# Gate matrix from one-hot products: fp32 operands against a power of two with a high and a low 16 bit part

## The chip, the cores and the metric

The kernel runs on one core of one Trainium2 chip. The metric is the device time of one execution in microseconds; the time before is the median of three runs, 961.69 us (960.93 to 962.33).

## What is computed

One decoder layer for 256 tokens of width 1024. The change lies in its last part, the product-key expert layer ("peer"). Each token gets 8 heads x 16 experts out of 128 x 128 with a gate for each:

```python
top_s, pos = lax.top_k(cand_s, PEER_TOPK)
experts = jnp.take_along_axis(cand_i, pos, axis=-1)
gates = jax.nn.softmax(top_s, axis=-1)
u = u_tab[ec]
a = jax.nn.gelu(jnp.einsum('td,thkd->thk', hc, u), approximate=False)
return jnp.einsum('thk,thkd->td', gc * a, v_tab[ec])
```

An expert's number is 128 x i1 + i2. For part of the tokens the kernel gathers the expert rows. For the others (176 of the 256) it computes all 16384 experts densely, and multiplies by a gate matrix W[i2, i1, token] that is zero except at the token's 128 experts.

## The kernel before

**Stages.** First the mixer (projections, retention, block attention, output projection), then the queries and keys of the experts, then a loop over 128 blocks of the table u (L1248 to L1282), then a loop over 128 blocks of the table v. Both tables stream through a ring of six 512 KB tiles on SyncE's queue.

**One step of the u loop** (block c): TensorE transposes block c + 2 (L737, eight 128x128 transposes), and ScalarE copies the result to SBUF (L738). TensorE multiplies block c with the hidden states (L1264, eight fp32 products of 128x128x128). Every second block ScalarE applies gelu (L1221, L1224), and GpSimd multiplies by the gates that exist by then (L1222). Then `gather` issues row fetches on GpSimd (L1028) and, a few steps later, their dots on VectorE (L1039). Last, `chain_step(BUDGET)` advances the side work by 1.5 us of its own planned costs: first the top-16 selection, then `dense_gates`, whose steps are booked with GSTEP = 1.6 each. So a group of four tokens is made for almost every block, 44 groups in all.

**A group of four tokens.** For token t let r run over its 128 (head, k) pairs on the partitions. With one-hot rows of i2 and of i1 the token's gate matrix is a product that contracts over r: W[:, :, t] = onehot(i2)^T (onehot(i1) x gate). `columns(t)` (L1170) transposes the indices and gates of 128 tokens, so that r lies on the partitions, and copies them from PSUM on ScalarE (`tT`, `tT1`). `one_hots` (L1145) builds, on VectorE, `o2`, an fp32 comparison of the negated iota with -i2 (L1152), and `o1b`, a bf16 comparison of `iota4` with i1 (L1154). Its `factors` (L1156) multiplies o1b by the gate on ScalarE, four activations for the four tokens (L1158), giving the fp32 `o1`. TensorE multiplies o2 by o1 for each token into one PSUM bank (L1192). `gates_evac` (L1201) writes the bank to W: for the blocks that are through, VectorE multiplies by what stands there (L1205), for the others ScalarE copies (L1207).

**What sets the order.** The order on each engine is that of the program (a manual schedule); engines meet at semaphores. In the step that builds group n, TensorE multiplies group n - 2 (LAG_G = 2), ScalarE makes the factors of group n - 1, and at the head of the next block the results of n - 2 are evacuated. The one-hots have three buffers in `oh_buf`, the factors and `o1b` two each, spread over `oh_buf` and `oh_more`; PSUM has two banks for the groups (`acc(1)`).

Of the kernel before, what the change touches and what calls it, by code (L numbers as in the profile page):

```python
# [11 lines left out]
F32 = mybir.dt.float32  # L12
F32R = mybir.dt.float32r
BF16 = mybir.dt.bfloat16
I16 = mybir.dt.int16
BF16 = mybir.dt.bfloat16
I32 = mybir.dt.int32
U32 = mybir.dt.uint32
AF = mybir.ActivationFunctionType
OP = mybir.AluOpType  # L20
AX = mybir.AxisListType

P = 128
S = 256
NT = S // P
D = 1024
KC = D // P
H = 8
NK = 128
# [6 lines left out]
NA = S - NG - NX  # L36
# [41 lines left out]
def layer_kernel(ctx, tc, x, mix_norm_g, w_in, ret_w_branch, moba_q_gain, moba_k_gain, moba_w_branch,  # L78
# [3 lines left out]
    V, A, G, T = nc.vector, nc.scalar, nc.gpsimd, nc.tensor  # L82
    ctx.enter_context(tc.manual_schedule())

    cp = ctx.enter_context(tc.tile_pool(name="cp", bufs=1))
# [708 lines left out]
    for t in range(NT):  # L794
        for q in range(2):
# [4 lines left out]
            p = side()  # L800
# [67 lines left out]
    i12f = tk.tile([P, NT, 2, NP], F32, name="i12f")  # L868
    oh_more = tk.tile([P, 2, 4, NK], F32, name="oh_more")
    iota4 = tk.tile([P, NK, 4], BF16, name="iota4")  # L870
    tT1 = tk.tile([P, NT, P], BF16, name="tT1")
    niota = tk.tile([P, P], F32, name="niota")
    tT = tk.tile([P, NT, 2, P], F32, name="tT")
    hTd = tk.tile([P, KC, NA], F32, name="hTd", tag="hx")
# [43 lines left out]
    def topk(t, q, s_sb):  # L918
# [57 lines left out]
        V.tensor_copy(i12f[:, t, 0, sl], i1i)  # L976
        V.scalar_tensor_tensor(i12f[:, t, 1, sl], i12f[:, t, 0, sl], float(NK), e1, op0=OP.mult, op1=OP.subtract)

# [137 lines left out]

    V.tensor_scalar(niota, iota, -1.0, None, op0=OP.mult)
    V.tensor_reduce(pick, ident.rearrange("p (h i) -> p i h", i=NXP), axis=AX.X, op=OP.add)
# [26 lines left out]
    def one_hots(oh_buf, t, k, n):  # L1145


        o2 = oh_buf[:, n % 3]
        o1 = (oh_buf[:, 3], oh_more[:, 0])[n % 2]
        o1b = oh_more[:, 1].rearrange("p a i -> p (a i)")[:, 256 * (n % 2):256 * (n % 2 + 1)].bitcast(BF16)  # L1150
        o1b = o1b.rearrange("p (i a) -> p i a", a=4)
        V.tensor_tensor(o2, niota[:, None, :].to_broadcast([P, 4, NK]), tT[:, t, 0, k:k + 4, None].to_broadcast([P, 4, NK]),  # L1152
                        op=OP.is_equal)
        V.tensor_tensor(o1b, iota4, tT1[:, t, None, k:k + 4].to_broadcast([P, NK, 4]), op=OP.is_equal)  # L1154

        def factors():  # L1156
            for j in range(4):
                A.activation(o1[:, j], o1b[:, :, j], AF.Copy, scale=tT[:, t, 1, k + j:k + j + 1])  # L1158

        return [(o2[:, j], o1[:, j]) for j in range(4)], factors  # L1160

# [6 lines left out]
    def dense_gates():  # L1168

        def columns(t):  # L1170
            p = side()
            for j, src in enumerate((i12f[:, t, 0], i12f[:, t, 1], gates[:, t])):
                T.transpose(p[:, j * P:(j + 1) * P], src, ident)
            A.activation(tT[:, t], p[:, P:3 * P].rearrange("p (j i) -> p j i", j=2), AF.Copy)  # L1174
            A.activation(tT1[:, t], p[:, :P], AF.Copy)

        oh_buf = cp.tile([P, 4, 4, NK], F32, name="oh_buf", tag="b8")
        yield 4.0
# [3 lines left out]
        for n0 in range(0, ND + 4 * LAG_G, 4):  # L1182
# [5 lines left out]
            if len(built) == LAG_G or (n0 >= ND and built):  # L1188
                n1, oh = built.pop(0)
                p = acc(1)  # L1190
                for j, (o2, o1) in enumerate(oh[0]):
                    T.matmul(p[:, j * P:(j + 1) * P], o2, o1, start=True, stop=True)  # L1192
                full.append((n1, p.rearrange("p (t i) -> p t i", t=4)))
# [106 lines left out]
    for c in range(NK):  # L1300
# [14 lines left out]
        if c == NK - 8:  # L1315
# [6 lines left out]
            r1 = hp_.tile([P, D], F32, name="rows", tag="hh", bufs=2)  # L1322
            r0b = oh_more.rearrange("p a b i -> p (a b i)")
            nc.gpsimd.dma_start(r0b[:P - NW], x1d[NW:, 0, :])
# [96 lines left out]
```

## Time and profile before

| | |
|---|---|
| median of three runs | 961.69 us |
| the profiled execution | 962.86 us |
| its span, first to last instruction | 961.1 us |
| granted TensorE clock, mean | 0.999 |
| TensorE matmul busy | 952.8 us (99%) |
| VectorE busy | 780.3 us (81%) |
| ScalarE busy | 527.3 us (55%) |
| GpSimd busy | 377.6 us (39%) |
| DMA | 320.40 MB, mean 333 GB/s |

In the profile PE is TensorE's matmuls and PEld its weight loads, DVE is VectorE, ACT ScalarE, POOL GpSimd, SP SyncE. L1192 is line 1192 of the kernel before. An fp32 product of this kernel stands as two MATMUL records with two LDWEIGHTS, a transpose as one of each. The record of a matmul is longer than its distance to the next one, because matmuls are pipelined; distances are read from start to start. A row of the waits reads: who waited, for whom, us in total, times, the longest. A row of a line reads: operation, count, shortest, median and longest duration in ns, first and last start in us.

### The profile page before, as it was taken

Reading aid. Unit: us, or ns where it says so; the run is one execution under the profiler, and the core shown is the slowest. Engines: PE = TensorE matmul, PEld = TensorE weight load, DVE = VectorE, ACT = ScalarE, POOL = GpSimd, SP = SyncE. Lnnn points to the kernel's source line nnn. Section 1 sums busy time; section 2 is a strip of 40 time slices with the busy share of each in tenths; the row PEclk is TensorE's granted clock in tenths of the full one; section 3 lists DMA queues with packets and bytes.
Section 4 is the critical chain, followed back from the end, with each engine's and each line's share of the span. In section 5 each row is a group of like instructions: output and inputs, shape, how many; then the busy total and the mean of one; then the engine's idle time right before and its main releaser. Section 6 shows DMA issues by size and latency. Waiting matters only on the chain.

```text
span 961.1 us, 19197 instructions
## 1 busy us (share of the span) xinstructions
PE 952.8 (99%) x7208; PEld 913.7 (95%) x7208; DVE 780.3 (81%) x1503; ACT 527.3 (55%) x954; POOL 377.6 (39%) x304
## 2 busy tenths in 40 slices
PE   9999999999999999999999999999999999999998
PEld 6877898998999999999999999999999999999997
DVE  6557667778679997999789998933988989898976
ACT  5544555534644445444577776975464545454543
POOL 3421000000203457344555676745635544564610
PEclk9999999999999999999999999999999999999999
DMA  9877779999798999999999999999999999999992
GB/s 313 229 196 219 232 222 295 302 278 278 251 385 322 410 365 343 402 363 388 370 392 367 354 359 373 368 332 358 350 377 383 385 381 410 366 407 380 409 338 82
DMA packets 109482, 320.40 MB, mean 333 GB/s; under 512 B 11436, under 2 KB 22581, under 8 KB 109262
## 3 DMA queue, kind: packets, MB, share of 16 engines
q1 hardware_dynamic: 64524, 184.43, 53.8%
q0 software_dynamic: 32528, 115.54, 32.4%
q10 hardware_dynamic: 12338, 19.21, 6.6%
q8 instruction: 57, 0.93, 0.4%
q14 instruction: 35, 0.29, 0.1%
HBM read 307.52 MB, written 13.14 MB: 334 GB/s over the span
## 4 chain that ended last, share of the span: by engine, by line
PE 94%; DVE 2%; ACT 1%; DMA 1%; issue 1%; POOL 1%; DVEq 0%; POOLq 0%; ACTq 0%
PE acc L1264 24%; PE side L737 10%; PE acc L1296 9%; PE side L1296 9%; PE acc L232 4%; PE acc L233 4%; PE acc L234 4%; PE acc L1192 4%; PE acc L1297 4%; PE side L1297 4%; PE acc L242 3%; PE acc L241 3%; PE acc L243 3%; PE side L1294 2%; PE acc L1294 1%; DMA bias<-skew 1%
## 5 line engine op out<-in xcount | busy, mean ns | idle before, releaser
L1028 POOL DMA_INDIRECT rows<-in_peer_u_dram,eg x86 | 105.3, 1224 | 75.2 <-DVE rows L1039 33.2
L1028 POOL DMA_INDIRECT rows<-in_peer_v_dram,eg x54 | 92.3, 1710 | 79.8 <-DVE vacc L1114 63.5
L737 PE MATMUL side<-ident,raw_ring 128*128 128x128 f32 x800 | 105.0, 274 | 0.0
L737 PEld LDWEIGHTS side<-ident,raw_ring 128*128 128x128 f32 x800 | 96.7, 190 | 0.0
L1236 ACT ACTIVATE cw<-W 128x352 fp32r<-128x352 f32 x58 | 28.8, 497 | 56.4 <-PE acc L1297 56.2
L1039 DVE SCALAR_TENSOR_TENSOR rows<-rows,h 128x1024 f32<-128x1024 f32 x43 | 51.9, 1217 | 5.3 <-DMA rows<-in_peer_u_dram,eg 5.3
L1114 DVE SCALAR_TENSOR_TENSOR vacc<-rows,av,vacc 128x1024 f32<-128x1024 f32 x43 | 55.0, 1279 | 0.1
L1237 DVE TENSOR_TENSOR cw<-W,cw 128x352 fp32r<-128x352 f32 x58 | 30.2, 520 | 22.7 <-ACT cw L1236 22.5
L1222 POOL TENSOR_TENSOR W<-W,gl 128x256 f32<-128x256 f32 (+16 forms) x29 | 25.6, 882 | 52.3 <-ACT gl L1221 49.0
L1207 ACT ACTIVATE W<-acc 128x512 f32<-128x512 f32 (+17 forms) x44 | 28.0, 635 | 32.9 <-DVE W L1205 27.0
L1152 DVE TENSOR_TENSOR oh_buf<-niota,tT 128x512 f32<-128x512 f32 x44 | 31.9, 725 | 5.6 <-ACT tT L1174 5.6
L580 POOL DMA_DIRECT2D x1d<-xt x1 | 0.7, 657 | 88.6 <-DVE xt L562 88.6
L1264 PE MATMUL acc<-hTd,raw_ring 128*128 128x128 f32 x256 | 31.2, 275 | 0.0
L156 POOL TENSOR_TENSOR gny<-va,minus_half 128x8 f32<-128x8 f32 x2 | 3.3, 1654 | 69.6 <-DVE va L454 69.6
L1205 DVE TENSOR_TENSOR W<-acc,W 128x280 f32<-128x280 f32 (+16 forms) x32 | 24.6, 769 | 7.2 <-PE acc L1192 5.3
L1264 PEld LDWEIGHTS acc<-hTd,raw_ring 128*128 128x128 f32 x256 | 29.9, 192 | 0.0
L1158 ACT ACTIVATE oh_buf<-oh_more,tT 128x128 f32<-128x128 bf16 x88 | 29.3, 423 | 0.0
L1158 ACT ACTIVATE oh_more<-oh_more,tT 128x128 f32<-128x128 bf16 x88 | 29.2, 419 | 0.0
L1192 PE MATMUL acc<-oh_buf 128*128 128x128 f32 x176 | 23.2, 275 | 0.0
L1192 PE MATMUL acc<-oh_more,oh_buf 128*128 128x128 f32 x176 | 23.2, 275 | 0.0
L1114 DVE SCALAR_TENSOR_TENSOR accx<-rows,av,accx 128x1024 f32<-128x1024 f32 x9 | 11.5, 1278 | 13.8 <-ACT accx L1111 12.0
L1192 PEld LDWEIGHTS acc<-oh_more,oh_buf 128*128 128x128 f32 x176 | 21.4, 192 | 0.0
(2698 smaller groups left out, 3507.9 us busy)
## 6 DMA issues: line engine op xcount, KB each, us to landing
raw_ring<-in_peer_v_dram SPq DMA_DIRECT2D x128, 512.0 KB
raw_ring<-in_peer_u_dram SPq DMA_DIRECT2D x100, 512.0 KB
raw_ring<-in_w_in_dram SPq DMA_DIRECT2D x52, 512.0 KB
raw_ring<-in_peer_w_q_dram SPq DMA_DIRECT2D x16, 512.0 KB
raw_ring<-turned SPq DMA_DIRECT2D x16, 512.0 KB
W<-in_peer_u_dram SPq DMA_DIRECT2D x12, 512.0 KB
eraw<-in_peer_u_dram ACTq DMA_DIRECT2D x32, 128.0 KB
h<-in_peer_u_dram ACTq DMA_DIRECT2D x32, 128.0 KB
```

The lines of the kernel that those rows point to most:

```text
L232: T.matmul(o[t], xh[:, s], wh, start=(k == 0), stop=False)
L233: T.matmul(o[t], xh[:, s], wl, start=False, stop=False)
L234: T.matmul(o[t], xl[:, s], wh, start=False, stop=(k == kc - 1))
L737: T.transpose(p[:, k * P:(k + 1) * P], r.rearrange("p (i k) -> p k i", k=KC)[:, 4 * q + k], ident)
L1028: G.indirect_dma_start(out=r, out_offset=None, in_=tab, in_offset=bass.IndirectOffsetOnAxis(ap=eg[:, j:j + 1], axis=0))
L1039: V.scalar_tensor_tensor(r, r, 1.0, h, op0=OP.mult, op1=OP.mult, accum_out=av[:, j:j + 1])
L1114: V.scalar_tensor_tensor(a, r, av[:, j:j + 1], a, op0=OP.mult, op1=OP.add)
L1158: A.activation(o1[:, j], o1b[:, :, j], AF.Copy, scale=tT[:, t, 1, k + j:k + j + 1])
L1192: T.matmul(p[:, j * P:(j + 1) * P], o2, o1, start=True, stop=True)
L1264: T.matmul(pa[:, n:n + NA], uT[:, k * P:(k + 1) * P], hT[:, k], start=(c % 2 == 0 and k == 0), stop=(k == KC - 1), skip_group_check=True)
L1296: T.matmul(o[b][:, :2 * ND], vh[:, n], w, start=(c == 0), stop=False, skip_group_check=True)
L1297: T.matmul(o[b][:, :ND], vl[:, n], w[:, :ND], start=False, stop=(c == NK - 1), skip_group_check=True)
```

## The change

The gate is written as a power of two times a rest. The power of two (`tS`, taken from the exponent bits) goes into one side: `factors` multiplies the one-hot of i1 by it, and the result is kept in bf16, exactly. The rest is split into a high fp16 part and a low fp16 part (`tM`), and the other side carries the one-hot of i2 times each of them. The gate matrix of a token is then the sum of two products of 16 bit operands, high and low, accumulated in PSUM (L1197 and L1198 of the kernel after, in place of L1192).

`one_hots` builds both one-hots in one fp16 comparison of 2 x 512 elements (`hot`, L1151) and multiplies the one of i2 by high and low in a second operation of 1024 elements (L1152). `columns` makes exponent, rest, high and low part with six operations of 128 elements on VectorE. The negated iota goes, the sign of i2 is turned where it is made, `iota4` and the indices become fp16. The buffers keep their sizes.

```diff
--- before.py
+++ after.py
@@ -866,11 +866,11 @@
     gg = tk.tile([P, NJ + NX], F32, name="gg")
     gates = tk.tile([P, NT, NP], F32, name="gates")
     i12f = tk.tile([P, NT, 2, NP], F32, name="i12f")
-    oh_more = tk.tile([P, 2, 4, NK], F32, name="oh_more")
-    iota4 = tk.tile([P, NK, 4], BF16, name="iota4")
-    tT1 = tk.tile([P, NT, P], BF16, name="tT1")
-    niota = tk.tile([P, P], F32, name="niota")
-    tT = tk.tile([P, NT, 2, P], F32, name="tT")
+    oh_more = tk.tile([P, 2, 2, NK, 4], F16, name="oh_more")
+    iota4 = tk.tile([P, NK, 4], F16, name="iota4")
+    tI = tk.tile([P, NT, 2, P], F16, name="tI")
+    tS = tk.tile([P, NT, P], F32, name="tS")
+    tM = tk.tile([P, NT, 2, P], F16, name="tM")
     hTd = tk.tile([P, KC, NA], F32, name="hTd", tag="hx")
     for q in range(2):
         A.activation(hTd[:, 4 * q:4 * q + 4], hTd_parts[q].rearrange("p (c t) -> p c t", c=4), AF.Copy)
@@ -974,7 +974,7 @@
         i1i = tk.tile([P, 2 * TOPK], I32, name="i1i")
         V.tensor_scalar(i1i, ei[:, t, sl], 7, None, op0=OP.logical_shift_right)
         V.tensor_copy(i12f[:, t, 0, sl], i1i)
-        V.scalar_tensor_tensor(i12f[:, t, 1, sl], i12f[:, t, 0, sl], float(NK), e1, op0=OP.mult, op1=OP.subtract)
+        V.scalar_tensor_tensor(i12f[:, t, 1, sl], i12f[:, t, 0, sl], -float(NK), e1, op0=OP.mult, op1=OP.add)
 
         V.tensor_tensor(gates[:, t, sl].rearrange("p (h k) -> p h k", h=2), ts_,
                         ts_[:, :, 0:1].to_broadcast([P, 2, TOPK]), op=OP.subtract)
@@ -1114,7 +1114,6 @@
                 V.scalar_tensor_tensor(a, r, av[:, j:j + 1], a, op0=OP.mult, op1=OP.add)
             gs["sum"] += 1
 
-    V.tensor_scalar(niota, iota, -1.0, None, op0=OP.mult)
     V.tensor_reduce(pick, ident.rearrange("p (h i) -> p i h", i=NXP), axis=AX.X, op=OP.add)
     V.tensor_copy(iota4, iota[:, :, None].to_broadcast([P, NK, 4]))
     held = list(HELD)
@@ -1145,19 +1144,18 @@
     def one_hots(oh_buf, t, k, n):
 
 
-        o2 = oh_buf[:, n % 3]
-        o1 = (oh_buf[:, 3], oh_more[:, 0])[n % 2]
-        o1b = oh_more[:, 1].rearrange("p a i -> p (a i)")[:, 256 * (n % 2):256 * (n % 2 + 1)].bitcast(BF16)
-        o1b = o1b.rearrange("p (i a) -> p i a", a=4)
-        V.tensor_tensor(o2, niota[:, None, :].to_broadcast([P, 4, NK]), tT[:, t, 0, k:k + 4, None].to_broadcast([P, 4, NK]),
-                        op=OP.is_equal)
-        V.tensor_tensor(o1b, iota4, tT1[:, t, None, k:k + 4].to_broadcast([P, NK, 4]), op=OP.is_equal)
+        hot = oh_more[:, n % 2]
+        o2 = oh_buf[:, n % 3].rearrange("p (w i a) -> p w i a", w=2, a=4)
+        o1 = oh_buf[:, 3, 512 * (n % 2):512 * (n % 2 + 1)].bitcast(BF16).rearrange("p (a i) -> p a i", a=4)
+        shape = [P, 2, NK, 4]
+        V.tensor_tensor(hot, iota4[:, None].to_broadcast(shape), tI[:, t, :, None, k:k + 4].to_broadcast(shape), op=OP.is_equal)
+        V.tensor_tensor(o2, hot[:, 1:2].to_broadcast(shape), tM[:, t, :, None, k:k + 4].to_broadcast(shape), op=OP.mult)
 
         def factors():
             for j in range(4):
-                A.activation(o1[:, j], o1b[:, :, j], AF.Copy, scale=tT[:, t, 1, k + j:k + j + 1])
-
-        return [(o2[:, j], o1[:, j]) for j in range(4)], factors
+                A.activation(o1[:, j], hot[:, 0, :, j], AF.Copy, scale=tS[:, t, k + j:k + j + 1])
+
+        return [(o2[:, 0, :, j], o2[:, 1, :, j], o1[:, j]) for j in range(4)], factors
 
     full = []
 
@@ -1171,10 +1169,17 @@
             p = side()
             for j, src in enumerate((i12f[:, t, 0], i12f[:, t, 1], gates[:, t])):
                 T.transpose(p[:, j * P:(j + 1) * P], src, ident)
-            A.activation(tT[:, t], p[:, P:3 * P].rearrange("p (j i) -> p j i", j=2), AF.Copy)
-            A.activation(tT1[:, t], p[:, :P], AF.Copy)
-
-        oh_buf = cp.tile([P, 4, 4, NK], F32, name="oh_buf", tag="b8")
+            g = tk.tile([P, 2, NA], F32, name="gl", bufs=2)
+            A.activation(g[:, 0], p[:, 2 * P:3 * P], AF.Copy)
+            A.activation(tI[:, t], p[:, :2 * P].rearrange("p (j i) -> p j i", j=2), AF.Copy)
+            V.tensor_scalar(tS[:, t].bitcast(I32), g[:, 0].bitcast(I32), 0x7F800000, None, op0=OP.bitwise_and)
+            V.tensor_scalar(tS[:, t], tS[:, t], 2.0 ** -100, 2.0 ** -10, op0=OP.max, op1=OP.mult)
+            V.tensor_scalar(g[:, 1].bitcast(I32), tS[:, t].bitcast(I32), -1.0, float(0x7F000000), op0=OP.mult, op1=OP.add)
+            V.tensor_tensor(g[:, 1], g[:, 0], g[:, 1], op=OP.mult)
+            V.tensor_copy(tM[:, t, 0], g[:, 1])
+            V.tensor_tensor(tM[:, t, 1], g[:, 1], tM[:, t, 0], op=OP.subtract)
+
+        oh_buf = cp.tile([P, 4, D], F16, name="oh_buf", tag="b8")
         yield 4.0
         columns(1)
         yield 0.1
@@ -1188,8 +1193,9 @@
             if len(built) == LAG_G or (n0 >= ND and built):
                 n1, oh = built.pop(0)
                 p = acc(1)
-                for j, (o2, o1) in enumerate(oh[0]):
-                    T.matmul(p[:, j * P:(j + 1) * P], o2, o1, start=True, stop=True)
+                for j, (hi, lo, o1) in enumerate(oh[0]):
+                    T.matmul(p[:, j * P:(j + 1) * P], hi, o1, start=True, stop=False)
+                    T.matmul(p[:, j * P:(j + 1) * P], lo, o1, start=False, stop=True)
                 full.append((n1, p.rearrange("p (t i) -> p t i", t=4)))
             if built:
                 built[-1][1][1]()
```

What it moves, on VectorE, where two groups are built. First before (oh_buf is the one-hot of i2, oh_more that of i1, W the gate matrix, rows a gathered row and its dot):

```order
L1152 TENSOR_TENSOR oh_buf<-niota,tT 128x512
L1154 TENSOR_TENSOR oh_more<-iota_2446,tT_2447 128x512
L1205 TENSOR_TENSOR W<-acc,W 128x4x76
L1039 SCALAR_TENSOR_TENSOR rows__5395,av<-rows__5395,rlo__3147 128x1024
L1152 TENSOR_TENSOR oh_buf<-niota,tT 128x512
```

And after, at the same place (oh_more is now both one-hots, oh_buf the one of i2 times high and low):

```order
L1151 TENSOR_TENSOR oh_more<-iota_2446,tI 128x1024
L1152 TENSOR_TENSOR oh_buf<-oh_more,tM 128x1024
L1211 TENSOR_TENSOR W<-acc,W 128x4x76
L1039 SCALAR_TENSOR_TENSOR rows__5417,av<-rows__5417,rlo__3146 128x1024
L1151 TENSOR_TENSOR oh_more<-iota_2446,tI 128x1024
```

The count and the places stay; the operations have 1024 elements, and the second one reads what the first one writes. On the same engine ahead of the first group, after `columns` (gl is a scratch tile, tS the power, tM high and low):

```order
L1175 TENSOR_SCALAR tS<-gl 128x128
L1176 TENSOR_SCALAR tS<-tS 128x128
L1177 TENSOR_SCALAR gl<-tS 128x128
L1178 TENSOR_TENSOR gl<-gl 128x128
L1179 CAST tM<-gl 128x128
L1180 TENSOR_TENSOR tM<-gl,tM 128x128
L1151 TENSOR_TENSOR oh_more<-iota_2446,tI 128x1024
```

Before, the first one-hots stood here with nothing ahead of them. On TensorE, between the products of one block and the next, before (side is a transpose, acc<-hTf the products with the hidden states):

```order
L1264 MATMUL acc<-hTf,rhi__5756 128x128 x8
L1192 MATMUL acc<-oh_more,oh_buf 128x128 x4
L737 MATMUL side<-ident,raw_ring 128x128 x8
L1264 MATMUL acc<-hTf,rhi__5799 128x128 x8
L1192 MATMUL acc<-oh_buf 128x128 x4
```

And after, the first of a group's four tokens and the start of the next:

```order
L737 MATMUL side<-ident,raw_ring 128x128 x8
L1270 MATMUL acc<-hTf,rhi__5221 128x128 x8
L1197 LDWEIGHTS oh_buf
L1197 MATMUL acc<-oh_buf 128x128
L1198 LDWEIGHTS oh_buf
L1198 MATMUL acc<-oh_buf 128x128
```

A token's one product becomes two, each with a weight load of its own; the place among the blocks is the same. ScalarE, GpSimd and SyncE keep their instructions in the same order, apart from the copies in `columns`, of which the gates' comes first now.

More of the change, by code (lines that the diff above doesn't have):

```diff
@@ L14 @@
 BF16 = mybir.dt.bfloat16
+F16 = mybir.dt.float16
 I16 = mybir.dt.int16
-BF16 = mybir.dt.bfloat16
 I32 = mybir.dt.int32
@@ L1322, in layer_kernel @@
             r1 = hp_.tile([P, D], F32, name="rows", tag="hh", bufs=2)
-            r0b = oh_more.rearrange("p a b i -> p (a b i)")
+            r0b = oh_more.rearrange("p a b i j -> p (a b i j)").bitcast(F32)
             nc.gpsimd.dma_start(r0b[:P - NW], x1d[NW:, 0, :])
```

## The prediction

> **What bounds the kernel now.** I read the page first, then the busy time by stretch, then the timeline and the waits of VectorE, since the change adds work there. The chain that ended last is TensorE's almost throughout:
>
> ```profile
> PE 94%; DVE 2%; ACT 1%; DMA 1%; issue 1%; POOL 1%; DVEq 0%; POOLq 0%; ACTq 0%
> PE acc L1264 24%; PE side L737 10%; PE acc L1296 9%; PE side L1296 9%; PE acc L232 4%; PE acc L233 4%; PE acc L234 4%; PE acc L1192 4%; PE acc L1297 4%; PE side L1297 4%; PE acc L242 3%; PE acc L241 3%; PE acc L243 3%; PE side L1294 2%; PE acc L1294 1%; DMA bias<-skew 1%
> ```
>
> The products that change (L1192) have 4% of it, 39 us. They run in one stage, from 478 to 642 us, beside the transposes of the u rows (L737), their products (L1264) and the dots of the gathered rows on VectorE (L1039). The stretches of this stage, and the one behind it:
>
> ```profile
> core 0: us, PE busy (x) PEld busy (x) DVE busy (x) ACT busy (x) POOL busy (x), PEclk, DMA share, GB/s
> 478.00:487.00 9.00, 9.00 (x83) 9.00 (x82) 7.93 (x15) 6.27 (x17) 5.24 (x4) 1.00 1.02 390
> 487.00:505.00 18.00, 18.00 (x164) 18.00 (x164) 16.58 (x31) 13.63 (x39) 8.51 (x8) 1.00 1.01 396
> 505.00:523.00 18.00, 18.00 (x164) 18.00 (x163) 16.14 (x30) 14.17 (x42) 10.20 (x10) 1.00 1.00 388
> 523.00:541.00 18.00, 18.00 (x164) 18.00 (x164) 16.55 (x31) 13.07 (x40) 12.80 (x12) 1.00 0.86 301
> 541.00:559.00 18.00, 18.00 (x164) 18.00 (x163) 17.26 (x31) 13.15 (x40) 11.44 (x11) 1.00 1.02 400
> 559.00:577.00 18.00, 18.00 (x163) 18.00 (x163) 17.36 (x30) 12.68 (x39) 12.90 (x13) 1.00 0.97 350
> 577.00:595.00 18.00, 18.00 (x164) 18.00 (x163) 15.67 (x27) 13.63 (x42) 11.68 (x11) 1.00 0.98 376
> 595.00:613.00 18.00, 18.00 (x163) 18.00 (x163) 15.64 (x27) 14.82 (x39) 13.16 (x11) 1.00 1.00 376
> 613.00:631.00 18.00, 18.00 (x164) 18.00 (x163) 17.73 (x32) 17.38 (x41) 11.47 (x10) 1.00 0.88 332
> 645.00:670.00 25.00, 25.00 (x227) 25.00 (x226) 8.47 (x7) 13.42 (x25) 12.61 (x12) 1.00 0.96 371
> ```
>
> TensorE is never idle, at a granted clock of 1.00. But VectorE is busy for 7.93+16.58+16.14+16.55+17.26+17.36+15.67+15.64+17.73 = 140.9 of the 153.0 us from 478 to 631. The stage has two engines close to full, and its second one has 12.1 us to spare. What it waited for:
>
> ```profile
> DVE W L1205 <- PE acc L1192: 5.3, 8, 1.4
> DVE rows L1039 <- DMA rows<-in_peer_u_dram,eg: 5.3, 5, 2.0
> DVE rows__6264 L1039 <- DMA rows__6264<-in_peer_u_dram,eg: 2.1, 1, 2.1
> DVE W L1205 <- issue: 1.1, 1, 1.1
> DVE W L1205 <- ACT oh_more L1158: 0.7, 1, 0.7
> ```
>
> So 5.3+1.1+0.7 = 7.1 us are waits for TensorE's results, ahead of the evacuation L1205, and the other 5.0 inside these stretches are gathered rows that had not landed.
>
> **The change part by part.** *TensorE.* A group of four tokens now takes four fp32 products, in future eight products of 16 bit operands (a high and a low half for each token).
>
> ```profile
> 540.67 1.05 PE L737 MATMUL side<-ident,raw_ring 128*128 128x128 f32 x8
> 541.55 1.95 PE L1264 MATMUL acc<-hTf,rhi__5799 128*128 128x128 f32 x16
> ...
> 543.34 1.06 PE L1192 MATMUL acc<-oh_buf 128*128 128x128 f32 x8
> 544.23 1.95 PE L1264 MATMUL acc<-hTf,rhi__5840 128*128 128x128 f32 x16
> ```
>
> From start to start a group takes 544.23−543.34 = 0.89 us, 0.223 for each token, in two records per fp32 product. The eight transposes before it take 541.55−540.67 = 0.88, 0.110 each, with 128 weight columns loaded for each. No 16 bit product stands in this trace. I bound it by a quarter of an fp32 product (0.056 us, if fp32 takes four passes, an estimate from 0.223) and by a transpose (0.110). A group then takes 0.45 to 0.88 us. I take 0.45, nearest to the row of the same operation, so that TensorE alone would win 44 × 0.44 = 19 us; both ends stay for the range. [...]
>
> *VectorE.* A group's one-hots were an fp32 comparison of 512 elements and a bf16 one of 512. They become a comparison of 1024 fp16 elements and a multiplication of 1024, which needs the comparison's result.
>
> ```profile
> L1152 DVE TENSOR_TENSOR oh_buf<-niota,tT x44: 675/685/1226, 478.0 to 630.2; 128x512 f32<-128x512 f32 x44
> ...
> L1154 DVE TENSOR_TENSOR oh_more<-iota,tT x44: 407/414/946, 478.6 to 630.8; 128x512 bf16<-128x512 bf16 x44
> ...
> L955 DVE TENSOR_TENSOR W<-W,ce x16: 601/605/610, 281.9 to 462.2; 128x864 int16<-128x864 int16 x16
> ```
>
> The two 16 bit rows give the slope: (605−414)/(864−512) = 0.543 ns per element, so 1024 elements take 605 + 160 × 0.543 = 692 ns. How operations follow one another:
>
> ```profile
> 547.67 0.68 DVE L1152 TENSOR_TENSOR oh_buf<-niota,tT 128x512 f32<-128x512 f32 x1
> 548.28 0.41 DVE L1154 TENSOR_TENSOR oh_more<-iota,tT 128x512 bf16<-128x512 bf16 x1
> 548.61 0.77 DVE L1205 TENSOR_TENSOR W<-acc,W 128x352 f32<-128x352 f32 x1
> ...
> 413.75 0.60 DVE L955 TENSOR_TENSOR W<-W,ce 128x864 int16<-128x864 int16 x1
> 414.38 1.05 DVE L957 TENSOR_REDUCE ef<-W 128x16 int16<-128x864 int16 x1
> ...
> 468.41 0.20 DVE L993 RECIPROCAL sm<-sm 128x8 f32<-128x8 f32 x1
> 468.65 0.29 DVE L994 TENSOR_TENSOR gates<-gates,sm 128x128 f32<-128x128 f32 x1
> ```
>
> Independent operations start 0.08 us before the one ahead has ended: the old pair costs 0.61 + 0.33 = 0.94 us. Where the second reads what the first wrote (L957 after L955) it starts 0.03 after the end. The new pair therefore costs 0.69 + 0.03 + 0.61 = 1.33 us, 0.39 more. Bounds: 0.28 more if the pair overlaps like the old one, 0.45 more if each takes 0.03 longer, my allowance for the collisions that the maxima of 1226 and 946 show. Over 44 groups 0.39 makes 17.2 us (12.3 to 19.8). The two calls that prepare gates and indices add six dependent operations of 128 elements, each between L993's 0.20 and L994's 0.29 and 0.03 apart, some 1.5 us a call, so 3.0 us. The dropped negated iota is one small operation outside the stage. Together VectorE gets 20.2 us more to do.
>
> *Beside these:* ScalarE's factors keep their count and shape (16 bit in, now 16 bit out); nothing moves on GpSimd or in SyncE's loads, and no transfer is added. The sign turned in the second index, the types of the iota and the buffers of equal size cost nothing.
>
> *The sum.* VectorE needs 140.9 + 20.2 = 161.1 us for what had 153.0. Its 7.1 us of waiting for TensorE vanish, since it is now the later one. Of the 5.0 us for gathered rows I keep 1.5, since a row has some 1.4 us more to land when VectorE is 0.39 slower in each of the three to four groups between its issue and its use. Its last one-hots (group 43) end later by 8.1 + 1.5 = 9.6 us. What TensorE makes of that:
>
> ```profile
> 597.10 0.42 DVE L1154 TENSOR_TENSOR oh_more<-iota,tT 128x512 bf16<-128x512 bf16 x1
> ...
> 600.75 1.06 PE L1192 MATMUL acc<-oh_buf 128*128 128x128 f32 x8
> ...
> 630.79 0.41 DVE L1154 TENSOR_TENSOR oh_more<-iota,tT 128x512 bf16<-128x512 bf16 x1
> ...
> 635.53 1.06 PE L1192 MATMUL acc<-oh_buf 128*128 128x128 f32 x8
> ...
> 641.77 1.06 PE L1192 MATMUL acc<-oh_more,oh_buf 128*128 128x128 f32 x8
> ```
>
> First bound: the last group's one-hots ended at 631.2 and its products began at 641.8, 10.6 us after. TensorE can be closer. Group 42's one-hots ended some 3.8 us (then 4.2) before group 43's; its products can follow about 1 us after them, once the factors are there; and from the products of 42 to those of 43 lie 641.77−635.53 = 6.24 us, then 5.8. That leaves about 3 us behind the last one-hots: 631.2 + 9.6 + 3 = 643.8, against 641.8 now, +2.0. Second bound: group 32 already follows its one-hots by only 600.75−597.52 = 3.2 us, which VectorE's evacuation and ScalarE's copies and factors fill. Up to there VectorE gets 33 × 0.39 + 3.0 = 15.9 us more and loses 7.1 of waits for TensorE and about 1.9 for rows, so TensorE is 6.9 us late at group 32; with 0.45 instead of 0.89 us a group it makes up 11 × 0.44 = 4.9 by group 43, again +2.0. Both are "not before"; for stalls that add up I take +2.5. Behind 645 TensorE is full with VectorE at 8.47 of 25 us, so the shift goes through to the end. The 19 us that TensorE saves are spent waiting for one-hots.
>
> The profiled execution took 962.86 us with a span of 961.1, the median of the three runs is 961.69; +2.5 on the median gives 964.2. About 0.2% (1.9 us) is what a measurement of this kernel can tell from no change.
>
> **The rivals.** *The weight loads eat TensorE's gain* (0.17). With 0.110 us a product a group takes 0.88, as now, and nothing is made up behind group 32: +6.8 us, 968.5. For it: every transpose in the trace takes 0.110, and each product here has its own load. Against: those loads are fp32. [...]
>
> *Faster: VectorE's pair overlaps* (0.20). If the multiplication starts 0.08 before the comparison ends, the addition is 0.28 a group, 12.3 + 3.0 = 15.3 us, and if no row is late either, VectorE ends at 631.2 + 156.2 − 153.0 = 634.4, TensorE's last group comes at 637.4, −4.4 us, 957.3. It decides below about 0.345 us more a group (2.0/44 less than 0.39). For it: L1152 and L1154 overlap so; against: they don't depend on each other, L955 and L957 do.
>
> *The fp16 operations don't run at the 16 bit rate* (0.04). By L952, int16 from fp32:
>
> ```profile
> L952 DVE TENSOR_TENSOR W<-iota,tf 128x864 int16<-128x864 f32 x16 | 16.9, 1055 | 0.2
> ```
>
> (1055−685)/352 = 1.05 ns an element makes 1.22 us each, 1.45 us more a group, 47 us more than summed: about 1011. Against it stands that L1154 and L955 have 16 bit operands with the same broadcasts.
>
> **How the numbers follow.** The forecast has 0.59, its own range 961 to 967.5 from the ends of VectorE's price and from 0 to 5.0 us of late rows. The range reaches from the faster rival (957.3) to past the slower one (969.5) and leaves the fourth case and the tails out. Faster by over 0.2%: most of the faster rival (0.16) and 0.03 of the forecast, 0.19. Within: 0.04 and 0.19, 0.23. Slower: the rest, 0.58.
>
> **What would show it.** Right: L1151 and L1152 near 0.69 us, the second after the first's end; VectorE busy for over 95% from 478 to 640; TensorE idle some 15 us in this stage, released by ScalarE's factors, which wait for VectorE; waits of L1211 for TensorE gone; the last one-hots near 641. Wrong: TensorE without idle time there and a stage 10 us or more shorter (VectorE did not bind), a pair clearly below 1.25 us, or idle time behind the stage that before did not have.

## The result, and the profile after

| | before | after |
|---|---|---|
| median, us (range, runs) | 961.92 (960.93 to 963.08, 6) | 969.31 (968.83 to 970.68, 6) |
| profiled execution, us (span) | 962.86 (961.1) | 968.83 (967.1) |

The changed kernel takes 1.0073 times as long (95% interval 1.0061 to 1.0086): 7.4 us more, where +2.5 was forecast. The chain that ended last, from the page of the changed kernel:

```profile
PE 76%; DVE 11%; DMA 5%; issue 3%; ACT 3%; POOL 2%; ACTq 0%; SPq 0%; DVEq 0%; POOLq 0%
PE acc L1270 15%; PE side L1302 8%; PE acc L1302 8%; PE side L737 7%; PE acc L232 5%; PE acc L233 5%; PE acc L234 5%; PE acc L1303 4%; PE side L1303 4%; PE acc L241 3%; PE acc L242 3%; PE acc L243 3%; DVE rows L1039 3%; DMA rows<-in_peer_u_dram,eg 2%; DVE W L1211 2%
```

VectorE has gone from 2% of the chain to 11%, and its dots (L1039) and evacuations (L1211) now stand there by name; TensorE has gone from 94% to 76%. The stretches of the stage and of what follows it:

```profile
core 0: us, PE busy (x) PEld busy (x) DVE busy (x) ACT busy (x) POOL busy (x), PEclk, DMA share, GB/s
478.00:487.00 9.00, 9.00 (x88) 9.00 (x87) 8.82 (x16) 5.01 (x13) 5.42 (x4) 1.00 1.01 388
487.00:505.00 18.00, 17.53 (x166) 16.35 (x164) 17.83 (x31) 13.39 (x38) 8.39 (x9) 1.00 0.99 379
505.00:523.00 18.00, 17.45 (x163) 16.40 (x162) 17.83 (x30) 14.18 (x42) 9.45 (x10) 1.00 0.97 382
523.00:541.00 18.00, 17.06 (x165) 16.74 (x164) 16.99 (x27) 11.78 (x35) 10.40 (x10) 1.00 0.93 326
541.00:559.00 18.00, 16.69 (x143) 15.89 (x143) 17.83 (x31) 13.43 (x42) 10.62 (x10) 0.91 0.95 359
559.00:577.00 18.00, 15.47 (x147) 14.52 (x147) 17.83 (x28) 11.03 (x35) 12.62 (x12) 1.00 0.95 340
577.00:595.00 18.00, 17.30 (x160) 16.38 (x159) 17.66 (x30) 12.45 (x38) 11.42 (x11) 1.00 0.94 352
595.00:613.00 18.00, 15.31 (x129) 14.42 (x128) 17.83 (x27) 11.63 (x34) 9.17 (x8) 0.91 0.76 279
613.00:631.00 18.00, 17.71 (x176) 17.24 (x175) 17.20 (x28) 18.00 (x44) 12.65 (x11) 1.00 0.97 368
645.00:660.00 15.00, 13.87 (x125) 13.48 (x124) 2.99 (x2) 11.76 (x24) 9.39 (x9) 1.00 0.83 297
```

From 478 to 631 VectorE is busy for 149.8 of 153.0 us, 98%, where it had 140.9. TensorE, never idle there before, now has 9.5 us without work, and in two stretches the clock that it was granted is 0.91. What TensorE and VectorE wait for, from 478 to 650 and from 478 to 645 us (waited for: us in total, times, longest):

```profile
PE acc L1197 <- ACT oh_buf L1156: 7.4, 8, 2.5
PE side L737 <- ACT rhi__7155 L738: 1.1, 1, 1.1
PE side L737 <- ACT rhi__5789 L738: 0.6, 1, 0.6
...
DVE rows L1039 <- DMA rows<-in_peer_u_dram,eg: 2.2, 3, 1.2
DVE av L1100 <- ACT av L1099: 0.3, 1, 0.3
```

VectorE's waits for TensorE's results are gone, and TensorE waits for the factors, which ScalarE makes out of VectorE's comparison. The new pair, first as all of its instances (times in ns, least, median, most), then in one place of the timeline (start, duration):

```profile
L1151 DVE TENSOR_TENSOR oh_more<-iota,tI x44: 675/687/1207, 477.8 to 639.4; 128x1024 f16<-128x1024 f16 x44
...
L1152 DVE TENSOR_TENSOR oh_buf<-oh_more,tM x44: 691/693/1341, 478.6 to 640.2; 128x1024 f16<-128x1024 f16 x44
```

```profile
537.90 0.69 DVE L1151 TENSOR_TENSOR oh_more<-iota,tI 128x1024 f16<-128x1024 f16 x1
538.62 0.69 DVE L1152 TENSOR_TENSOR oh_buf<-oh_more,tM 128x1024 f16<-128x1024 f16 x1
```

The second starts 0.03 us after the first has ended. The next operation (L1211) starts at 539.23, so that the pair costs 1.33 us. And the end of the stage:

```profile
639.32 0.22 PE L1197 MATMUL acc<-oh_buf 128*128 128x128 bf16 x1
639.38 0.22 PE L1198 MATMUL acc<-oh_buf 128*128 128x128 bf16 x1
...
640.17 0.69 DVE L1152 TENSOR_TENSOR oh_buf<-oh_more,tM 128x1024 f16<-128x1024 f16 x1
...
644.45 0.26 ACT L1099 ACTIVATE av<-av 128x64 f32<-128x64 f32 x1 [3.73 <-DVE rows L1039]
644.62 1.31 ACT L1156 ACTIVATE oh_buf<-oh_more,tS 128x128 bf16<-128x128 f16 x4
...
645.17 0.22 PE L1197 MATMUL acc<-oh_buf 128*128 128x128 bf16 x1
...
647.32 1.19 PE L737 MATMUL side<-ident,raw_ring 128*128 128x128 f32 x8 [1.06 <-ACT rhi__7155 L738]
```

The last one-hots end at 640.86 (631.2 before), the last group's products begin at 645.17 (641.77 before). By the timeline, the v loop begins at 675.01 (670.21 before), and the span ends 6.0 us later.

### The profile page after: what moved, and what is told of

Its sections match the earlier page's. It is cut to its first block, busy times and chain, and to the rows that moved or that the text cites. A ratio compares the mean times of both kernels' runs of the same rounds, so it can differ in the third digit from the quotient of the medians.

```text
span 967.1 us, 19134 instructions
## 1 busy us (share of the span) xinstructions
PE 947.5 (98%) x7208; PEld 902.1 (93%) x7208; DVE 799.9 (83%) x1514; ACT 526.7 (54%) x954; POOL 376.3 (39%) x304
## 4 chain that ended last, share of the span: by engine, by line
PE 76%; DVE 11%; DMA 5%; issue 3%; ACT 3%; POOL 2%; ACTq 0%; SPq 0%; DVEq 0%; POOLq 0%
PE acc L1270 15%; PE side L1302 8%; PE acc L1302 8%; PE side L737 7%; PE acc L232 5%; PE acc L233 5%; PE acc L234 5%; PE acc L1303 4%; PE side L1303 4%; PE acc L241 3%; PE acc L242 3%; PE acc L243 3%; DVE rows L1039 3%; DMA rows<-in_peer_u_dram,eg 2%; DVE W L1211 2%
## 5 line engine op out<-in xcount | busy, mean ns | idle before, releaser
L1028 POOL DMA_INDIRECT rows<-in_peer_v_dram,eg x54 | 95.0, 1759 | 80.2 <-DVE vacc L1114 64.2
L737 PE MATMUL side<-ident,raw_ring 128*128 128x128 f32 x800 | 108.6, 280 | 1.7 <-ACT rhi__7155 L738 1.1
L1156 ACT ACTIVATE oh_buf<-oh_more,tS 128x128 bf16<-128x128 f16 x176 | 58.7, 426 | 0.2 <-DVE oh_more L1151 0.2
L1039 DVE SCALAR_TENSOR_TENSOR rows<-rows,h 128x1024 f32<-128x1024 f32 x43 | 53.0, 1245 | 1.4 <-DMA rows<-in_peer_u_dram,eg 1.4
L1228 POOL TENSOR_TENSOR W<-W,gl 128x256 f32<-128x256 f32 (+16 forms) x29 | 23.5, 809 | 61.4 <-ACT gl L1227 56.6
L1243 DVE TENSOR_TENSOR cw<-W,cw 128x352 fp32r<-128x352 f32 x58 | 30.2, 521 | 12.8 <-ACT cw L1242 12.7
L1197 PE MATMUL acc<-oh_buf 128*128 128x128 bf16 x176 | 30.0, 221 | 8.9 <-ACT oh_buf L1156 7.4
L1152 DVE TENSOR_TENSOR oh_buf<-oh_more,tM 128x1024 f16<-128x1024 f16 x44 | 33.3, 756 | 2.2
L1198 PEld LDWEIGHTS <-oh_buf 128*128 128x128 f16 x176 | 19.9, 114 | 14.4 <-issue 7.9
L1151 DVE TENSOR_TENSOR oh_more<-iota,tI 128x1024 f16<-128x1024 f16 x44 | 32.1, 730 | 0.0
L1198 PE MATMUL acc<-oh_buf 128*128 128x128 bf16 x176 | 30.2, 223 | 0.0
L1211 DVE TENSOR_TENSOR W<-acc,W 128x280 f32<-128x280 f32 (+16 forms) x32 | 24.6, 768 | 0.0
```

Of the source, the lines that this page charges most:

```text
L737: T.transpose(p[:, k * P:(k + 1) * P], r.rearrange("p (i k) -> p k i", k=KC)[:, 4 * q + k], ident)
L1028: G.indirect_dma_start(out=r, out_offset=None, in_=tab, in_offset=bass.IndirectOffsetOnAxis(ap=eg[:, j:j + 1], axis=0))
L1039: V.scalar_tensor_tensor(r, r, 1.0, h, op0=OP.mult, op1=OP.mult, accum_out=av[:, j:j + 1])
L1156: A.activation(o1[:, j], hot[:, 0, :, j], AF.Copy, scale=tS[:, t, k + j:k + j + 1])
L1198: T.matmul(p[:, j * P:(j + 1) * P], lo, o1, start=False, stop=True)
```

## The experiments

The theory: VectorE's time for each group, with the path from its comparison over ScalarE's factors to the products, sets the stage, and the shorter products are worth almost nothing here. The rivals: TensorE loses the time itself (its clock, the loads, the weights' column step), the gathered rows are the bound, or only the order of the operations is. Each result is a median and its ratio to the kernel before on the same chip, with a 95% interval. Differences in us between two runs are differences of medians; by the intervals they are good to about 2 us.

**The products twice.** Each pair of products is issued twice, so that a group takes TensorE 0.89 us from start to start (539.11 to 540.00), as before the change:

```diff
-                    T.matmul(p[:, j * P:(j + 1) * P], hi, o1, start=True, stop=False)
-                    T.matmul(p[:, j * P:(j + 1) * P], lo, o1, start=False, stop=True)
+                    for _ in range(2):
+                        T.matmul(p[:, j * P:(j + 1) * P], hi, o1, start=True, stop=False)
+                        T.matmul(p[:, j * P:(j + 1) * P], lo, o1, start=False, stop=True)
```

> Every pair of products of the kernel after is issued twice (the second pair starts over, so W is the same): TensorE has 0.89 us a group again, as in the kernel before, VectorE is as after. Theory 1, VectorE sets the pace and TensorE's saving serves only to catch up behind the last groups: 2 to 5 us more than after, 971 to 974 us, with VectorE as full as after. Theory 2, the idle gaps lower TensorE's clock and that is most of the loss: the gaps are filled, the clock stays at 1.00 and the time falls to 963 to 967 us.

Measured: 971.40 us, 1.0100 (1.0083 to 1.0117). TensorE got 44 × 0.44 = 19 us more work, and the kernel takes only 2.1 us longer than the changed one, as the first theory has it. The stretches that bear on it:

```profile
541.00:559.00 18.00, 17.86 (x197) 17.61 (x196) 17.23 (x29) 12.84 (x40) 9.24 (x10) 1.00 1.00 382
...
595.00:613.00 18.00, 15.97 (x168) 15.56 (x167) 17.83 (x27) 11.72 (x34) 9.20 (x8) 1.00 0.79 291
```

The granted clock is 1.00 where the changed kernel had 0.91, and the time is no better. That speaks against the clock as the cause of the loss, but does not settle it, since this run also has more work where the changed kernel catches up; the next run leaves that part out. With TensorE's work as it was, the change costs the 9.0 us between this run and the kernel before.

**The products twice in groups 0 to 27.** Of the same edit, one line differs:

```diff
-                    for _ in range(2):
+                    for _ in range(2 if n1 < 112 else 1):
```

> The products are doubled for the first 28 of the 44 groups only, where TensorE waits anyway, so that it can still catch up at the end. Theory 1: no change from after within 1 us, 968.5 to 970.3 us, since only idle time is filled. Theory 2, the clock: the first of the two stretches with a clock of 0.91 goes, 1.5 to 3 us less than after, 966 to 968 us.

Measured: 970.58 us, 1.0093 (1.0070 to 1.0116), just above the theory's range and not to be told from the changed kernel. The same two stretches:

```profile
541.00:559.00 18.00, 18.00 (x198) 17.78 (x198) 17.83 (x29) 13.29 (x42) 10.68 (x10) 1.00 0.97 361
595.00:613.00 18.00, 14.52 (x132) 13.49 (x132) 17.83 (x27) 11.83 (x34) 8.67 (x8) 1.00 0.81 300
```

The clock is 1.00 in both (a slower one, 0.89, comes from 645 to 660 us instead), and the time is not shorter: the rival of the clock falls. More work on TensorE in the first 28 groups costs nothing that these runs resolve.

**The kernel before with a longer pair.** Nothing of the change; the 16 bit comparison of each group stands twice:

```diff
         V.tensor_tensor(o1b, iota4, tT1[:, t, None, k:k + 4].to_broadcast([P, NK, 4]), op=OP.is_equal)
+        V.tensor_tensor(o1b, iota4, tT1[:, t, None, k:k + 4].to_broadcast([P, NK, 4]), op=OP.is_equal)
```

> The kernel before, its products unchanged, with the 16 bit comparison of each group issued twice: 0.41 - 0.08 = 0.33 us (up to 0.41) more on VectorE in 44 groups, 14.5 to 18 us. Theory 'VectorE's added work sets the time of the changed kernel': the last one-hots end 4 to 10 us later and TensorE, which here can't make up time with shorter products, loses as much as it starves: 966 to 973. Rival 'VectorE hides beside TensorE, and the loss comes from the new products or their clock': 961 to 964.

Measured: 967.66 us, 1.0057 (1.0040 to 1.0074). The fp32 products are all there and the granted clock is 1.00 from 478 to 645 us, so VectorE's addition alone brings a loss of 5.3 us. In this run's table of groups (busy, mean ns, idle before) the added comparison and the evacuations:

```profile
L1155 DVE TENSOR_TENSOR oh_more<-iota,tT 128x512 bf16<-128x512 bf16 x44 | 20.3, 461 | 1.5
...
L1206 DVE TENSOR_TENSOR W<-acc,W 128x280 f32<-128x280 f32 (+16 forms) x32 | 24.4, 762 | 0.0
```

The evacuations, L1205 in the kernel before, had waited 7.1 us and wait no longer: VectorE is full, busy for 151.3 of the 153.0 us from 478 to 631. The last one-hots end at 639.1, 7.9 us later.

**Without the multiplication.** Both products of a token take the bare one-hot:

```diff
-        hot = oh_more[:, n % 2]
-        o2 = oh_buf[:, n % 3].rearrange("p (w i a) -> p w i a", w=2, a=4)
+        hot = oh_buf[:, n % 3].rearrange("p (w i a) -> p w i a", w=2, a=4)
...
-        V.tensor_tensor(o2, hot[:, 1:2].to_broadcast(shape), tM[:, t, :, None, k:k + 4].to_broadcast(shape), op=OP.mult)
```

> The second operation of the pair, the multiplication by high and low part, is left out, and both products of a token take the bare one-hot of i2 (so the gates lack the rest beside their power of two); TensorE has the same eight products a group. Theory 1, VectorE's added work binds: VectorE has 0.61 us a group instead of 0.94 before, its stage needs some 130 us, TensorE binds again and keeps its 0.44 us a group, so the time falls to about 19 us below the kernel before: 940 to 946 us. Theory 2, the loss comes from TensorE's clock after idle gaps or from the six operations in columns: still 955 us or more.

Measured: 956.91 us, 0.9946 (0.9930 to 0.9962). The sign is the first theory's and its size is missed by 11 us; by the number alone the second theory (955 or more) could stand. VectorE's waits show another bound:

```profile
DVE rows L1039 <- DMA rows<-in_peer_u_dram,eg: 16.0, 12, 4.3
```

These are waits for gathered rows, 2.2 us in the changed kernel, and some in other buffers come on top; from 505 to 523 and from 541 to 559 the DMA share is 1.02. Here VectorE, busy for 16.44 and 15.47 of the 18 us of these stretches (17.83 in both in the changed kernel), has time to spare and asks for rows before they have landed.

**The same, with fewer rows in the stage.** The dots' paces change in this stage and in the v loop, so that 0.16 × 44 = 7 dots move:

```diff
-GATHER_V = 0.62
+GATHER_V = 0.68
...
-GATHER_G = 1.36
+GATHER_G = 1.2
```

> The multiplication is left out as in the run without it (both products of a pair take the bare one-hot, so the gates lack the parts), and in addition the dot products ask for fewer gathered rows per group (pace 1.2 instead of 1.36 in the gates' stage, 0.68 instead of 0.62 in the v loop). Without the multiplication VectorE waited 16.0 us for gathered rows in 12 waits, at a DMA share of 1.02 to 1.03 in two windows. Theory 'rows': the transfer of gathered rows is what bounds the stage once VectorE has time; 0.16 dots fewer per group are 7 of 60 rows, the row waits fall below about 5 us, the time goes to 943 to 952. Rival 'TensorE': the 956.9 of the run without the multiplication comes from TensorE's own work, row waits may fall but the time stays at 955 to 959.

Measured: 949.88 us, 0.9878 (0.9862 to 0.9895), within the range of the theory of rows. The six operations in `columns` and a stretch with a clock of 0.91 (577 to 595 us) are here as in the run before, so at most a part of the 11 us missing there is theirs: 7.0 went with the rows that moved. The largest group of waits for rows did not fall as far as expected, though:

```profile
DVE rows L1039 <- DMA rows<-in_peer_u_dram,eg: 10.8, 8, 2.8
DVE W L1209 <- PE acc L1196: 10.3, 15, 1.0
```

Up to the last one-hots, with the rows in all buffers counted, they fell from 19.9 to 8.7 us; behind them TensorE waits for nothing more in this stage. VectorE now waits 10.3 us for TensorE, which itself waits 2.5. TensorE is the bound again, with groups of products half as long, and only here do 12.2 of the 19 us that they save arrive. A dot that moves takes its work on VectorE away with its row, so how much is due to either stays open.

**The multiplication one step later.** That of the group before is issued ahead of a group's comparison, so that ScalarE's factors run while VectorE does other work:

```diff
-        V.tensor_tensor(o2, hot[:, 1:2].to_broadcast(shape), tM[:, t, :, None, k:k + 4].to_broadcast(shape), op=OP.mult)
+        def parts():
+            V.tensor_tensor(o2, hot[:, 1:2].to_broadcast(shape), tM[:, t, :, None, k:k + 4].to_broadcast(shape), op=OP.mult)
...
+                if built[-1][0] == n0 - 4:
+                    built[-1][1][2]()
```

> The multiplication of group n - 1 is issued ahead of the comparison of group n, so that the two stand next to each other without depending on each other; all counts and results are those of after. Theory 1: the pair costs 0.61 + 0.61 = 1.22 us instead of 1.33, 44 x 0.11 = 4.8 us less than after, 963.5 to 966 us. Theory 2: TensorE's gaps shrink a little, 967 to 969.5 us.

Measured: 963.75 us, 1.0017 (1.0005 to 1.0029), 5.6 less than the changed kernel with the same operations on every engine, and within the first theory's range. The edit does two things at once. It shortens the pair, from 1.33 to 1.21 us where the multiplication starts at 602.95 and the operation behind the comparison at 604.16, and it lets the products follow sooner. Group 32 shows the second; first the changed kernel, then this one:

```profile
604.00 0.87 DVE L1211 TENSOR_TENSOR W<-acc,W 128x408 f32<-128x408 f32 x1
606.06 1.32 ACT L1156 ACTIVATE oh_buf<-oh_more,tS 128x128 bf16<-128x128 f16 x4
606.51 0.22 PE L1197 MATMUL acc<-oh_buf 128*128 128x128 bf16 x1
606.81 0.22 PE L1197 MATMUL acc<-oh_buf 128*128 128x128 bf16 x1
607.12 0.22 PE L1197 MATMUL acc<-oh_buf 128*128 128x128 bf16 x1
607.43 0.22 PE L1197 MATMUL acc<-oh_buf 128*128 128x128 bf16 x1
```

```profile
602.95 0.68 DVE L1154 TENSOR_TENSOR oh_buf<-oh_more,tM 128x1024 f16<-128x1024 f16 x1
...
603.76 0.22 PE L1199 MATMUL acc<-oh_buf 128*128 128x128 bf16 x1
```

In the changed kernel the group's one-hots have ended at 604.08, just as L1211 starts, but ScalarE, with copies that wait for L1211 queued ahead, starts the factors only at 606.06, and four of them take 1.32 us, so the tokens' products follow 0.31 us apart: 1.03 us from the first to the transposes at 607.54, instead of 0.44. With the late multiplication the first product follows it by 603.76 − 603.63 = 0.13 us, and from there to the transposes it takes 0.80 us.

How far VectorE itself comes forward, by the last comparison of the stage, first in the changed kernel, then here:

```profile
639.38 0.69 DVE L1151 TENSOR_TENSOR oh_more<-iota,tI 128x1024 f16<-128x1024 f16 x1
```

```profile
637.09 0.68 DVE L1151 TENSOR_TENSOR oh_more<-iota,tI 128x1024 f16<-128x1024 f16 x1
```

It is 2.3 us earlier, although VectorE waits 6.2 us for rows from 478 to 645 us instead of 2.2. So the 5.6 us hold both the shorter pair and the closer following, and no run here separates the two.

**The changed kernel with the paces alone**, the same two constants.

> The changed kernel with the paces 1.2 and 0.68 alone, the multiplication where the change put it. Theory 'VectorE bounds the stage': 7 dots fewer in it are 8.6 us less work on VectorE, so the last one-hots end at 632 to 634 instead of 640.9 and the time falls by 6 to 9 us, to 960 to 963. Rival 'the late factors bound it' (TensorE waits for the chain multiplication, factors, products of each group, whatever VectorE's sum is): 966 to 970.

Measured: 961.87 us, 1.0002 (0.9983 to 1.0020), as the theory of VectorE's work has it; the last one-hots end at 631.3. 8.6 us less work for VectorE in the stage are 7.4 us of time. TensorE still waits 5.5 us for factors.

**Both**, the late multiplication and the paces 1.2 and 0.68.

> The multiplication of a group is issued one step later, as in the earlier run (963.75 us), and the paces are 1.2 and 0.68 as well: 0.16 x 44 = 7 dots, about 8.6 us of VectorE's work at 1.22 us each, move out of the gates' stage into the v loop. Theory 'VectorE bounds the stage': the last one-hots end some 8 us earlier, TensorE's own stream becomes the next bound, 953 to 959. Rival 'only the order mattered' (the earlier gain came from the wait that the late multiplication took away, and VectorE's sum of work is not the bound): 962 to 965. If VectorE is then short of time in the v loop instead: 960 to 966 with longer waits for VectorE's columns there.

Measured: 956.33 us, 0.9958 (0.9932 to 0.9983): faster than both kernels, and by the medians 13.0 us less than the changed one, the sum of 5.6 and 7.4 within what the intervals can tell. The two cures add up, so the order of the operations is not all of it, and neither is the number of dots.

**The kernel before with the paces**, as a control.

> The kernel before with the paces 1.2 and 0.68 alone. Theory 'TensorE bounds the stage before': no change, 960 to 964. Rival 'VectorE or the rows bound it before already': 953 to 958.

Measured: 963.22 us, 1.0015 (0.9995 to 1.0035). There was nothing to win: TensorE was the bound, as the prediction read it.

**Both, with fewer dots still** (on the late multiplication and the paces 1.2 and 0.68):

```diff
-GATHER_V = 0.68
+GATHER_V = 0.74
...
-GATHER_G = 1.2
+GATHER_G = 1.04
```

> The later multiplication with the paces 1.04 and 0.74, so that another 7 dots leave the stage. Theory 'VectorE bounds the stage until TensorE is full': of the 9.4 us that TensorE waited for one-hots with paces 1.2 and 0.68 most go, the dots lie in the v loop where VectorE has time: 948 to 953. Rival 'the next bound is reached': 955 to 958 (the dots that moved are late for what follows the v loop, or gathered rows collide there).

Measured: 974.35 us, 1.0119 (1.0097 to 1.0140): both expectations missed, 18 us above the paces 1.2 and 0.68. (The 9.4 us of the expectation add the waits of TensorE's weight loads, 5.0, to those of its products, 4.4, which are largely the same time.) In the stage TensorE hardly waits for one-hots any more, but for the gates themselves:

```profile
PE side L1173 <- DMA gates<-gx: 10.9, 1, 10.9
PE acc L1199 <- DVE oh_buf L1154: 0.2, 1, 0.2
```

L1173 transposes the gates for the second call of `columns`; they come from dots that were put off too far. So the dots have a due time inside the stage. From 577 to 595 us the granted clock is 0.72. The v loop, too, has a wait of 7.2 us of TensorE for VectorE (L1307 for L150). What share each has of the 18 us stays open.

**Compare and multiply in one instruction.** The side of the parts is built by eight operations of 128 elements, in one piece for each token instead of with a step of four columns; the index and the parts are kept in fp32 for it:

```diff
-        V.tensor_tensor(hot, iota4[:, None].to_broadcast(shape), tI[:, t, :, None, k:k + 4].to_broadcast(shape), op=OP.is_equal)
-        V.tensor_tensor(o2, hot[:, 1:2].to_broadcast(shape), tM[:, t, :, None, k:k + 4].to_broadcast(shape), op=OP.mult)
+        V.tensor_tensor(hot, iota4, tI[:, t, None, k:k + 4].to_broadcast([P, NK, 4]), op=OP.is_equal)
+        for j in range(4):
+            for w in range(2):
+                V.tensor_scalar(o2[:, w, j], iota16, tI2[:, t, k + j:k + j + 1], tM[t][:, w, k + j:k + j + 1], op0=OP.is_equal, op1=OP.mult)
```

> The side that carries the parts is built by eight tensor_scalar operations per group on 128 elements each (compare with the index, multiply by the part, in one instruction) instead of half of the comparison and the multiplication of 1024 elements; the comparison that is left has 512 elements. Theory 'VectorE's time per group bounds the stage': the time follows the new pair's cost. At about 0.1 us per operation the pair costs 0.33 + 0.8 = 1.13 us instead of 1.33, some 9 us less in 44 groups, 960 to 963; at about 0.2 us each it costs 1.9 us, 25 us more, 990 to 998. Rival 'the weights' column step of four elements holds up TensorE' (here they lie in one piece): the products start less than 0.055 us apart.

Measured: 1001.92 us, 1.0410 (1.0393 to 1.0428). One group of it:

```profile
539.98 1.91 DVE L1156 TENSOR_SCALAR oh_buf<-iota,tI,oh_more 128x128 f16<-128x128 f16 x8
541.09 0.22 PE L1204 MATMUL acc<-oh_buf 128*128 128x128 bf16 x1
541.14 0.22 PE L1205 MATMUL acc<-oh_buf 128*128 128x128 bf16 x1
...
541.80 0.70 DVE L1218 TENSOR_TENSOR W<-acc,W 128x328 f32<-128x328 f32 x1
```

The eight take 541.80 − 539.98 = 1.82 us, 0.228 each, and the comparison that is left takes 0.34 to the next start in one place (544.70 to 545.04; 0.52 ahead of the eight above), so the pair costs about 2.16 us, 0.83 more than the changed kernel's 1.33. In 44 groups that makes 36.5 us, and 32.6 are measured: VectorE's time per group goes almost wholly into the time. The products of weights in one piece start 0.055 us apart, as those with the column step do, so the rival that blamed the step falls.

## Why the prediction was right, and where its size was off

The measured 969.31 us lies above the forecast's own range (961 to 967.5). Only the range that was drawn past the rival of the weight loads (968.5) reached so far, and that rival did not come true: that the time still lies within the whole range is luck. The bound and the direction are not.

*The bound and VectorE's terms* were right. The pair costs 1.33 us, as summed; VectorE's waits for TensorE are gone; the stage's last one-hots end 9.66 us later, where 9.6 was forecast. That the two meet so closely is partly luck: the first call of `columns` ran ahead of the stage, where VectorE had waited before (the first comparison begins at 477.76, before at 477.97), and added nothing, while the second took 2.57 us (591.94 to 594.51) instead of 1.5.

*TensorE's product* took 0.055 us with a load of its own (the eight of group 42 start between 639.32 and 639.71), where 0.056 was taken: a quarter of the 0.223 us of an fp32 product. The four passes behind the 0.056 were an assumption that no trace shows; the two times are what the runs show. The rival of the weight loads, with the 0.110 us of a transpose for each product, was wrong as well. The doubled products show that the saving of 19 us is worth about 2 us here (971.40 against 969.31).

*The rivals.* The pair did not overlap (its second operation starts 0.03 us after the end of the first), and the fp16 operations ran at the rate of the 16 bit rows: 0.687 and 0.693 us at the median, where 0.692 was taken and the rival had 1.22.

*The step that failed* is the one that asked what TensorE makes of the late one-hots: "+2.0", taken as +2.5. The last group's products came 3.4 us later than before, not 2.0; both of its bounds were too near:

- "Group 32": 6.9 us of lateness were forecast and 5.8 measured (606.51 against 600.75), but of the 4.9 us that TensorE was to make up by group 43 it made up 2.4. The step had TensorE free of VectorE behind group 32. By the timeline it waited until group 37, whose products at 622.85 are 5.2 us late. Each such group was also stretched by factors that arrive 0.31 us apart, so its products did not take the 0.45 us of the sum.
- "Its products can follow about 1 us after them": group 42's one-hots ended at 637.03, and its products began at 639.32, 2.3 us after them, since TensorE was full from 622.85 on (busy for 14.00 of the 14.00 us from 631 to 645). The 5.8 us from there to group 43 are as forecast (645.17 − 639.32 = 5.85).

*The shift goes through to the end*: it did, and grew on the way. The transposes behind the last group waited 1.06 us (the row at 647.32) because ScalarE had stood 3.73 us at L1099, behind VectorE's last dots, with the factors and copies queued behind it; the v loop thus begins 4.8 us late. Another 1.2 us come by the end, 0.7 of them TensorE's waits for VectorE's copies at L1243 in the v loop. That is 6.0 us in the profiled executions. The other 1.4 us to the 7.4 of the medians are which execution was profiled: that of before lies 0.94 us above its median, that of after 0.48 below.

The idle 15 us forecast for TensorE were 9.5 in the stretches, because part of its waiting lies between the products of a group and part in slower clocked work. The two cures take off 7.4 us (less work on VectorE) and 5.6 us (a later multiplication). The prediction had a term for the work; for the way from the one-hots to the products it had only "about 3 us behind the last one-hots", and nothing for what the late factors cost inside each group.

## What to carry to other kernels

Where a change shortens work on the engine that bounds a stage and lengthens work on one that is 92% busy there, sum the second engine first; here what was saved on the first was mostly spent waiting (of 19 us, about 2 counted). Read also how near the consumer can follow: the chain over ScalarE's queue, which began the factors of group 32 at 606.06 though its one-hots had ended at 604.08, cost time here that no engine's sum shows. Issuing an operation a step later, beside one that it does not depend on, won 5.6 us here with the same operations, by a shorter pair and a closer following together. Moving other work out of the stage helped (7.4 us for 7 dots) until it met its own due time, and then the time was longer at once (+18 us for the last 0.16 dots a group).

## What the runs showed of the hardware that was not expected

TensorE ran slower behind some short pauses and not behind others. In the changed kernel, with the idle time before an instruction in brackets:

```profile
542.10 0.22 PE L1197 MATMUL acc<-oh_buf 128*128 128x128 bf16 x1 [1.41 <-ACT oh_buf L1156]
543.13 3.02 PE L1270 MATMUL acc<-hTf,rhi__5906 128*128 128x128 f32 x16
...
545.94 0.31 PE L1197 MATMUL acc<-oh_buf 128*128 128x128 bf16 x1
546.05 0.31 PE L1198 MATMUL acc<-oh_buf 128*128 128x128 bf16 x1
```

After 1.41 us without work and a group with products 0.3 us apart, sixteen products that take 1.95 us elsewhere take 3.02, and the next group's start 0.11 us apart instead of 0.055: half the rate, for some 3.5 us (between 543.13 and the transposes at 546.79), at a granted clock of 0.91 in the stretch. The longest pause of TensorE in the changed kernel's stage, 2.54 us ahead of 598.40, lies in the other stretch with 0.91. A pause of 1.57 us at 571.96 was not followed by a lower clock in its stretch (1.00), and with the paces alone neither was one of 2.29 us at 592.55, so the length of the pause alone does not decide it; what else does, these runs do not settle.

The same number of elements took VectorE longer in eight small operations here: the eight of 128 elements that compare and multiply in one instruction took 0.228 us each from start to start, 1.82 together, while one multiplication of 1024 elements takes 0.69.
